# Experts' transpositions in two groups per expert instead of four, the next expert's places worked out a stage earlier, the last output scattered in two halves

## The chip, the cores and the metric

One core of one Trainium2 chip runs the kernel. The metric is the device time of one execution in microseconds; three timed executions of the kernel before gave 1836.58 to 1839.4 us with a median of 1838.2 us.

## The reference

One layer over 1024 tokens of width 1024: a modulated RMS norm, a projection to 2576 columns, an mLSTM mixer and a dilated attention mixer beside each other, an output projection with a gated residual, and then the part that this change concerns:

```
h2 = rms_norm(x, norm2_g) * (1 + scale2) + shift2
affinity = softmax(h2 @ w_router + b_router)
gates, idx = top_k(affinity.T, 128)             # each of 16 experts chooses 128 of 1024 tokens
xin = h2[idx]                                   # 128 x 1024 for each expert
hid = silu(xin @ w_gate) * (xin @ w_up)         # 128 x 2048
y = (hid @ w_down) * gates
out = x + gate2 * zeros.at[idx].add(y)
```

All is float32. Each expert has three weight matrices of 8 MB, so 403 MB are read from device memory for the 16 experts.

## The kernel before, in words

The first 680 us or so compute the mixers, the router and the choice of tokens. The rest, `phase_experts` (L1584), goes through the 16 experts one after the other, and the change lies wholly in it.

**The products.** A weight matrix comes in eight pieces of 128 x 2048 numbers through a ring of buffers, loaded by the SP queue (`feed`, L1474 and L1476). ScalarE rounds a piece to the matrix type (`wh`, L1489) and VectorE takes the rest (`wl`, L1505), so that three products, of the rounded input with `wh`, of the input's rest with `wh` and of the rounded input with `wl`, give nearly float32. `mm` (L1510) issues the 12 matmuls of a piece (L1524), each 128 x 128 by 128 x 512, and then the next cut. There are four buffers each for `wh` and `wl`, and the cut runs about three pieces ahead in the written order. An expert has 24 pieces: 8 for `w_gate`, 8 for `w_up`, 8 for `w_down`, together 288 matmuls.

**The order of the stages.** While expert e is in hand, TensorE does gate(e), up(e), and then down(e-1), which is one expert late. PSUM is two sets of four banks, `px` and `py`, whose roles change with each expert: gate(e) fills set X, up(e) fills set Y, down(e-1) uses two banks of X.

**What stands between the products.** Three small jobs are put between pieces. `expert_hT` (L1556) turns one quarter of the previous expert's hidden rows, by four 128 x 128 transpositions on TensorE (L1564) and a split on ScalarE (L124) and VectorE (L125); it is called after pieces 1, 3, 5 and 7 of gate. `expert_xT` (L1530) turns half of the next expert's gathered rows by four transpositions (L1538), four ScalarE scalings (L1544) and a split; it is called after pieces 2 and 4 of down. `route_expert` (L1429) finds the next expert's places: VectorE writes a one-hot table (`onehot`, L1426), TensorE does eight narrow products (L1437), VectorE makes the list of rows and the gates (L1441 to L1443), and GpSimd starts an indirect DMA that gathers the rows into `xin` (L1445). Its first part follows piece 0 of up, its second part piece 2 of up.

**The output.** At the end of down, VectorE writes the gated result over `xin` in two halves of 512 columns (L1580), and GpSimd starts an indirect DMA that adds its 128 rows of 4 KB to `out` (L1581). `xin` is one buffer: the next gather waits until this scatter has read it, and each scatter to `out` is ordered behind the landing of the one before it, since their rows are known only at run time. At the very end, down of the last expert runs alone and its scatter is the last work of the program.

**What sets the order in the queues.** The functions state an order, but a planner fixes each engine's instruction list before the program runs. It goes through the instructions with assumed costs and takes, whenever an engine is free, the ready one that comes first in the written order; so a transposition whose input is ready can be moved ahead of a product whose weights are not, by its assumed times. The `wl` cuts and the one-hot table keep their written order among themselves (`keep_in_program_order`). On the chip every engine then takes its list strictly in order. The transpositions and places of which the prediction speaks are such instructions.

Of the kernel before, what the change touches and what calls it, by code (L numbers as in the profile page):

```python
# [14 lines left out]
I32 = mybir.dt.int32  # L15
AF = mybir.ActivationFunctionType
OP = mybir.AluOpType
# [3 lines left out]
P = 128  # L21
# [8 lines left out]
NE = 16  # L30
# [16 lines left out]
FEEDS = (2, 8, 14, 20, 26, 32)  # L47
LATE = 3
CUTS = 4
HT = (1, 3, 5, 7)  # L50
PAIR0 = 2, 4, 5
MIX = 8
SORTS = {9: (0, 3), 24: (3, 2), 39: (5, 2)}
# [53 lines left out]
class K:  # L107
# [1045 lines left out]
    def phase_out(self):  # L1153
# [4 lines left out]
        with ExitStack() as st:  # L1158
# [55 lines left out]
            for k in range(MH):  # L1214
                if k == MH - 1:
                    for _ in merge:
                        pass
                prep(k)
                if k == 1:
                    for i in range(NT):  # L1220
                        x_load(i)
                for n in range(2 * G1):
                    mm(pss[n], n // 2, n % 2, k)
                    next(consts, 1)
                    if n % 2:
                        next(merge, 1)
# [23 lines left out]
            for i in range(G1, NT):  # L1250
                for c in range(2):
                    ps = psum()
                    for k in range(MH):
                        mm(ps, i, c, k)
                        step += 1
                        for g in todo.pop(step, ()):
                            g()
                        if step in SORTS:
                            side.append(self.route_sort(*SORTS[step]))
                        if step in FEEDS:  # L1260
                            self.feed()
                        pump(PUMP)
                    epilogue(i, c, ps)
                if i < NT - 1:
                    finish(i, self.out_norm(i, 1, ss), (step + TAIL[0], step + TAIL[1]))
# [163 lines left out]
    def route_expert(self, e, psum):  # L1429

        nc, rt = self.nc, self.rt
        if e:
            self.onehot(e, self.slot)
        oh = self.oh
        ps = psum()
        for i in range(NT):
            nc.tensor.matmul(ps[:, :5], oh[:, i], self.R[:, i, e], start=(i == 0), stop=(i == NT - 1))  # L1437
        yield
        idx = rt.tile([P, 1], I32, name="idx", bufs=3)
        rg = rt.tile([P, 5], F32, name="rg", bufs=3)  # L1440
        nc.vector.tensor_copy(rg, ps[:, :5])  # L1441
        nc.vector.scalar_tensor_tensor(idx, rg[:, 0:1], float(P), rg[:, 1:2], op0=OP.mult, op1=OP.add)
        nc.vector.tensor_reduce(rg[:, 0:1], rg[:, 2:5], axis=AX.X, op=OP.add)  # L1443
        xin = self.xin
        nc.gpsimd.indirect_dma_start(out=xin, out_offset=None, in_=self.h2_d,  # L1445
                                     in_offset=bass.IndirectOffsetOnAxis(ap=idx[:, :1], axis=0))
        yield dict(idx=idx, gate=rg[:, 0:1], xin=xin)
# [62 lines left out]
    def mm(self, xs, n, first, last):  # L1510

        nc = self.nc
        w, l = self.ready.pop(0)
        (xh, xl), ps = xs, n
        N = len(ps) * 512
        prods = (xh, w), (xl, w), (xh, l)
        order = [(q, t, c) for q in range(3) for t in range(FF // N) for c in range(len(ps))]
        if last and not (self.fed or self.halves or self.ready):

            order.sort(key=lambda a: (a[1], a[0], a[2]))  # L1520
        for q, t, c in order:
            x, y = prods[q]
            o = t * N + c * 512
            nc.tensor.matmul(ps[c], x[:, t], y[:, o:o + 512], start=first and q == 0 and t == 0, stop=last and (q, t) == (2, FF // N - 1))  # L1524
        if self.ahead:
            self.ahead -= 1
        else:
            self.cut()
# [36 lines left out]
        self.split(h, l, ps.rearrange("p (k n) -> p k n", k=4))  # L1565
        u.setdefault("hT", []).append((h, l))

    def expert_down(self, u, psum):

        nc = self.nc  # L1570
        ps = [psum() for _ in range(2)]
        for i in range(8):
            h, l = u["hT"][i // 2]
            k = slice(2 * (i % 2), 2 * (i % 2) + 2)
            self.mm((h[:, k], l[:, k]), ps, i == 0, i == 7)
            yield i
        y = self.xin
        for c in range(2):
            t = slice(c * 512, (c + 1) * 512)
            nc.vector.scalar_tensor_tensor(y[:, t], ps[c], u["gate"], self.gate2[:, t], op0=OP.mult, op1=OP.mult)  # L1580
        nc.gpsimd.indirect_dma_start(out=self.out, out_offset=bass.IndirectOffsetOnAxis(ap=u["idx"][:, :1], axis=0),  # L1581
                                     in_=y, in_offset=None, compute_op=OP.add)

    def phase_experts(self):  # L1584


        nc = self.nc
        sets = [lambda: self.psx.tile([P, 512], F32, name="px"), lambda: self.psy.tile([P, 512], F32, name="py")]

        self.hid = self.m2.tile([P, FF], F32, name="hid")  # L1590
        self.xT = (self.sort_mem, self.m1.tile([P, KT, P], F32R, name="xTh", bufs=2),
                   self.yp.tile([P, KT, P], F32R, name="xTl", tag="og", bufs=MH))
        half = lambda pool, tag, **kw: pool.tile([P, D], F32, name="w_half", tag=tag, **kw)
        og = lambda: half(self.yp, "og", bufs=MH)
        self.feed([self.hid], once=True)
        self.feed([half(self.m1, t, bufs=2) for t in ("xTh", "xin")])
        self.xin = self.m1.tile([P, D], F32, name="xin", bufs=2)
        for _ in range(2):
            self.feed([half(self.yap, "ya", bufs=MH) for _ in range(2)], once=True)
        late = [None] * (RING - EARLY) + [[og(), og()], [og(), half(self.m2, "w_x")]]  # L1600
        for t in late[:-LATE]:
            self.feed(t)
        _, u = self.route_expert(0, sets[1])
        for t in late[-LATE:]:
            self.feed(t, nc.gpsimd)
        for _ in range(CUTS - 1):
            self.cut()
        for b in range(2):
            self.expert_xT(u, b, sets[1], True)
        self.started = True  # L1610
        self.ahead = 1
        self.cut()
        p = None
        for e in range(NE):
            X, Y = sets[e % 2], sets[1 - e % 2]
            n = None
            for i in self.expert_up(u, "w_gate", X):
                if p and i in HT:
                    self.expert_hT(p, HT.index(i), Y)
            u["hid"] = hid = self.m2.tile([P, FF], F32, name="hid")  # L1620
            for c in range(4):
                nc.scalar.activation(hid[:, c * 512:(c + 1) * 512], u["ps_w_gate"][c], AF.Silu)  # L1622
            for i in self.expert_up(u, "w_up", Y):
                if e + 1 < NE and i == 0:
                    route = self.route_expert(e + 1, X)
                    next(route)
                if e + 1 < NE and i == 2:
                    n = next(route)
            for c in range(4):
                t = slice(c * 512, (c + 1) * 512)  # L1630
                nc.vector.tensor_mul(hid[:, t], hid[:, t], u["ps_w_up"][c])
            if p:
                for i in self.expert_down(p, X):
                    if n and i in (2, 4):
                        self.expert_xT(n, i // 2 - 1, Y)
                    if e == NE - 1 and i in (2, 4, 6):
                        self.expert_hT(u, i // 2 - 1, Y)
            elif n:
                for b in range(2):
                    self.expert_xT(n, b, Y)  # L1640
            p, u = u, n
        self.expert_hT(p, 3, Y)
        for _ in self.expert_down(p, Y):
            pass


# [100 lines left out]
```

## Time and profile before

| | |
|---|---|
| median of three timed executions | 1838.2 us (1836.58 to 1839.4) |
| the profiled execution: its own time, its span | 1833.95 us, 1832.0 us |
| TensorE matmul busy, over the span | 1722.9 us (94%) |
| VectorE busy | 1487.1 us (81%) |
| ScalarE busy | 1197.7 us (65%) |
| GpSimd busy | 180.5 us (10%) |
| DMA | 517.26 MB, mean 282 GB/s |
| mean granted TensorE clock | 0.982 of full |

The shares are means over the mixers, the router and the experts together. In the page's 40 slices the experts are the last 25: TensorE shows 9 tenths or more in nearly all of them, VectorE 8 or 9, ScalarE 6 or 7, and the DMA engines 9. Three engines and the DMA are all near their limit there, so what bounds an expert has to be read from the waits inside it.

### The profile page before, as it was taken

What the parts mean: (1) busy time and instruction counts of PE and PEld (TensorE: products, weight loads), DVE (VectorE), ACT (ScalarE), POOL (GpSimd) and SP (SyncE); (2) the same over time, 40 slices, a digit from 0 to 9 for tenths busy, and PEclk for the clock granted to TensorE, in tenths of its full rate; (3) what the DMA queues carried; (4) which work ended last, traced back from release to release, by engine and by line L of the source; (5) the groups of instructions that cost most, each with busy time, mean ns of one, the idle gap of its engine ahead of it and who ended that gap; (6) DMA issues with size and microseconds to landing.
All of it is one profiled execution on the core that took longest, in us unless ns stands there. A gap on an engine that the chain in (4) does not pass through costs nothing. (4 is left out here: it accounts for less than half of the span.)

```text
span 1832.0 us, 24429 instructions
## 1 busy us (share of the span) xinstructions
PE 1722.9 (94%) x8696; PEld 1402.8 (77%) x8696; DVE 1487.1 (81%) x2156; ACT 1197.7 (65%) x1603; POOL 180.5 (10%) x185
## 2 busy tenths in 40 slices
PE   5999999989998939999999999999999999999997
PEld 4777888778886827888888778777787777777785
DVE  5578885687866788988988898888898888888886
ACT  5346454377763537787777777776776776777764
POOL 1001000031123020010110000100000001001000
PEclk9999999999999959999999999999999999999999
DMA  9135663325557768999999999999999999999892
GB/s 325 42 114 172 213 215 98 110 80 116 135 129 227 258 255 336 359 354 382 410 363 345 373 345 379 372 335 390 352 369 384 357 364 387 329 382 368 311 391 67
DMA packets 152553, 517.26 MB, mean 282 GB/s; under 512 B 33163, under 2 KB 50833, under 8 KB 116721
## 3 DMA queue, kind: packets, MB, share of 16 engines
q1 hardware_dynamic: 138560, 478.92, 70.7%
q0 software_dynamic: 10960, 36.32, 7.5%
q8 instruction: 68, 1.11, 0.2%
q10 hardware_dynamic: 2912, 0.48, 0.2%
q14 instruction: 53, 0.43, 0.1%
HBM read 488.16 MB, written 27.50 MB: 281 GB/s over the span
## 5 line engine op out<-in xcount | busy, mean ns | idle before, releaser
L1505 DVE TENSOR_TENSOR wl<-w,wh 128x2048 fp32r<-128x2048 f32 x278 | 627.8, 2285 | 81.6 <-ACT wh L1489 81.2
L1489 ACT ACTIVATE wh<-w 128x2048 fp32r<-128x2048 f32 x278 | 523.1, 1919 | 55.2 <-PE py L1524 26.3
L1505 DVE TENSOR_TENSOR wl<-w_half,wh 128x1024 fp32r<-128x1024 f32 x210 | 245.6, 1217 | 8.6 <-ACT wh L1489 8.5
L1489 ACT ACTIVATE wh<-w_half 128x1024 fp32r<-128x1024 f32 x210 | 211.8, 1058 | 24.1 <-PE px L1524 13.1
L1524 PE MATMUL py<-wl,xTh 128*128 128x512 f32 x512 | 139.9, 394 | 7.7 <-DVE wl L1505 7.7
L1524 PE MATMUL px<-wl,xTh 128*128 128x512 f32 x512 | 139.7, 394 | 4.5 <-DVE wl L1505 4.5
L1524 PE MATMUL px<-wh,xTh 128*128 128x512 f32 x512 | 141.1, 395 | 2.3 <-ACT xTh L124 2.1
L1524 PE MATMUL py<-wh,xTh 128*128 128x512 f32 x512 | 140.8, 394 | 2.2 <-ACT wh L1489 2.0
L1524 PE MATMUL py<-wh,xTl 128*128 128x512 f32 x512 | 138.3, 390 | 0.0
L1524 PE MATMUL px<-wh,xTl 128*128 128x512 f32 x512 | 138.1, 391 | 0.0
L1524 PE MATMUL px<-wh,hT 128*128 128x512 f32 x512 | 130.4, 396 | 0.1
L1524 PE MATMUL py<-wh,hT 128*128 128x512 f32 x512 | 129.0, 393 | 0.0
L1524 PEld LDWEIGHTS py<-wl,xTh 128*128 128x128 f32 x512 | 94.6, 188 | 33.4 <-DVE wl L1505 14.6
L1524 PEld LDWEIGHTS px<-wl,xTh 128*128 128x128 f32 x512 | 95.0, 188 | 29.5 <-DVE wl L1505 10.4
L1524 PEld LDWEIGHTS px<-wh,xTh 128*128 128x128 f32 x512 | 95.3, 189 | 23.9 <-ACT xTh L124 2.5
L1524 PEld LDWEIGHTS py<-wh,xTh 128*128 128x128 f32 x512 | 94.7, 188 | 24.0 <-ACT wh L1489 4.5
L1524 PEld LDWEIGHTS px<-wh,hT 128*128 128x128 f32 x512 | 95.6, 190 | 22.1 <-ACT wh L1489 2.1
L1524 PEld LDWEIGHTS px<-wh,xTl 128*128 128x128 f32 x512 | 96.7, 189 | 20.6
L1524 PEld LDWEIGHTS py<-wh,xTl 128*128 128x128 f32 x512 | 96.0, 188 | 20.4 <-DVE xTl L125 0.2
L1524 PEld LDWEIGHTS py<-wh,hT 128*128 128x128 f32 x512 | 95.0, 188 | 20.8 <-ACT wh L1489 0.7
L1581 POOL DMA_INDIRECT out_dram<-xin,idx x16 | 48.3, 3019 | 590.6 <-DVE xin L1580 590.6
L1445 POOL DMA_INDIRECT xin<-h_d,idx x16 | 37.8, 2362 | 477.9 <-DVE rg L1443 197.4
(456 smaller groups left out, 3138.2 us busy)
## 6 DMA issues: line engine op xcount, KB each, us to landing
w<-in_w_down_dram SPq DMA_DIRECT2D x95, 1024.0 KB, 8.4
w<-in_w_gate_dram SPq DMA_DIRECT2D x91, 1024.0 KB, 7.2
w<-in_w_up_dram SPq DMA_DIRECT2D x88, 1024.0 KB, 7.1
w_half<-in_w_gate_dram SPq DMA_DIRECT2D x70, 512.0 KB, 7.6
w_half<-in_w_up_dram SPq DMA_DIRECT2D x70, 512.0 KB, 7.5
w_half<-in_w_down_dram SPq DMA_DIRECT2D x66, 512.0 KB, 8.3
ada_w<-in_w_ada_dram SPq DMA_DIRECT2D x64, 256.0 KB, 3.5
wraw<-in_w_in_dram SPq DMA_DIRECT2D x20, 512.0 KB, 4.3
```

Source lines behind the costliest of these rows:

```text
L1445: nc.gpsimd.indirect_dma_start(out=xin, out_offset=None, in_=self.h2_d, in_offset=bass.IndirectOffsetOnAxis(ap=idx[:, :1], axis=0))
L1489: act = self.nc.scalar.activation(h[:, j * m:(j + 1) * m], t, AF.Copy)
L1505: self.tc.keep_in_program_order(self.nc.vector.tensor_sub(l[:, c], t, h[:, c]))
L1524: nc.tensor.matmul(ps[c], x[:, t], y[:, o:o + 512], start=first and q == 0 and t == 0, stop=last and (q, t) == (2, FF // N - 1))
L1581: nc.gpsimd.indirect_dma_start(out=self.out, out_offset=bass.IndirectOffsetOnAxis(ap=u["idx"][:, :1], axis=0), in_=y, in_offset=None, comp ...
```

## The change

`HT` becomes a table from piece to quarters: after piece 3 of gate the quarters 0 and 1 of the previous hidden rows are turned, after piece 6 the quarters 2 and 3. Both halves of the next input are turned after piece 3 of down. The one-hot table of the next expert is written after piece 1 of gate instead of after piece 0 of up, its eight products come after piece 3 of gate, right behind the first group of transpositions and in the other PSUM set, and the row list and the gather after piece 5 of gate instead of piece 2 of up. For the last expert all four quarters are turned inside down of the one before, after its pieces 3 and 6, where a quarter had come after it. In the very last piece the 12 products are sorted by output half first, and each half of the result is scattered by a DMA of its own, 128 rows of 2 KB each, to the row numbers 2*idx and 2*idx+1 of `out` seen as 2048 half rows; VectorE makes these numbers.

```
-HT = (1, 3, 5, 7)
+HT = {3: (0, 1), 6: (2, 3)}
...
     def route_expert(self, e, psum):
-        if e:
-            self.onehot(e, self.slot)
...
-            order.sort(key=lambda a: (a[1], a[0], a[2]))
+            order.sort(key=lambda a: (a[2], a[0], a[1]))
...
-    def expert_down(self, u, psum):
+    def expert_down(self, u, psum, last=False):
...
             nc.vector.scalar_tensor_tensor(y[:, t], ps[c], u["gate"], self.gate2[:, t], op0=OP.mult, op1=OP.mult)
-        nc.gpsimd.indirect_dma_start(out=self.out, ...)
+            if last:
+                row = self.rt.tile([P, 1], I32, name="idx", bufs=3)
+                nc.vector.tensor_scalar(row, u["idx"], 2.0, float(c), op0=OP.mult, op1=OP.add)
+                nc.gpsimd.indirect_dma_start(out=self.out.rearrange("s (h n) -> (s h) n", h=2), ..., in_=y[:, t], compute_op=OP.add)
+        if not last:
+            nc.gpsimd.indirect_dma_start(out=self.out, ...)
...
             for i in self.expert_up(u, "w_gate", X):
-                if p and i in HT:
-                    self.expert_hT(p, HT.index(i), Y)
+                if p:
+                    for b in HT.get(i, ()):
+                        self.expert_hT(p, b, Y)
+                if e + 1 < NE and i == 1:
+                    self.onehot(e + 1, self.slot)
+                if e + 1 < NE and i == 3:
+                    route = self.route_expert(e + 1, Y)
+                    next(route)
+                if e + 1 < NE and i == 5:
+                    n = next(route)
...
-            for i in self.expert_up(u, "w_up", Y):
-                if e + 1 < NE and i == 0:
-                    route = self.route_expert(e + 1, X)
-                    next(route)
-                if e + 1 < NE and i == 2:
-                    n = next(route)
+            for _ in self.expert_up(u, "w_up", Y):
+                pass
...
                 for i in self.expert_down(p, X):
-                    if n and i in (2, 4):
-                        self.expert_xT(n, i // 2 - 1, Y)
-                    if e == NE - 1 and i in (2, 4, 6):
-                        self.expert_hT(u, i // 2 - 1, Y)
+                    if n and i == 3:
+                        for b in range(2):
+                            self.expert_xT(n, b, Y)
+                    if e == NE - 1:
+                        for b in HT.get(i, ()):
+                            self.expert_hT(u, b, Y)
...
-        self.expert_hT(p, 3, Y)
-        for _ in self.expert_down(p, Y):
+        for _ in self.expert_down(p, Y, True):
             pass
```

## Rows read from the trace of the kernel before

**Rows 1.** Busy time by stretch, one expert each, with its header

```profile
core 0: us, PE busy (x) PEld busy (x) DVE busy (x) ACT busy (x) POOL busy (x), PEclk, DMA share, GB/s
865.18:934.05 68.87, 68.87 (x321) 56.81 (x320) 63.68 (x48) 54.17 (x51) 7.20 (x2) 1.00 0.99 383
...
1148.63:1220.63 72.00, 70.52 (x322) 56.42 (x320) 62.65 (x47) 53.27 (x49) 5.91 (x2) 1.00 0.96 364
...
1651.86:1727.76 75.90, 72.58 (x323) 57.49 (x321) 62.02 (x48) 51.73 (x49) 5.91 (x2) 0.98 0.92 343
```

**Rows 2.** Waits from 780 to 1780 us: total us, times, longest

```profile
DVE wl L1505 <- ACT wh L1489: 80.5, 50, 5.5
...
ACT wh L1489 <- DMA w_half<-in_w_gate_dram: 0.8, 1, 0.8
```

**Rows 3.** TensorE's timeline: start us, us, ..., count; the expert from 934 us

```profile
939.50 0.63 PE L1564 MATMUL py<-ident,hid 128*128 128x128 f32 x4
939.88 1.17 PE L1524 MATMUL px<-wh,xTh 128*128 128x512 f32 x4
940.89 1.08 PE L1524 MATMUL px<-wh,xTl 128*128 128x512 f32 x4
941.81 1.08 PE L1524 MATMUL px<-wl,xTh 128*128 128x512 f32 x4
...
967.42 0.35 PE L1437 MATMUL px<-route_rhs,oh 128*128 128x5 bf16 x8
967.63 0.71 PE L1524 MATMUL py<-wh,xTl 128*128 128x512 f32 x2
968.18 1.09 PE L1524 MATMUL py<-wl,xTh 128*128 128x512 f32 x4
```

**Rows 4.** TensorE's timeline, down and the next gate, from 1126 us

```profile
1125.99 1.03 PE L1538 MATMUL py<-ident,xin 128*128 128x128 f32 x8
1126.78 2.09 PE L1524 MATMUL px<-wh,hT 128*128 128x512 f32 x8
1128.70 0.75 PE L1564 MATMUL px<-ident,hid 128*128 128x128 f32 x5
...
1151.60 1.19 PE L1524 MATMUL py<-wl,xTh 128*128 128x512 f32 x4 [0.99 <-DVE wl L1505]
```

**Rows 5.** TensorE's timeline, two places where it waits for gathered rows

```profile
1554.87 0.52 PE L1538 MATMUL py<-ident,xin 128*128 128x128 f32 x3 [1.55 <-DMA xin<-h_d,idx]
...
1700.34 1.29 PE L1538 MATMUL py<-ident,xin 128*128 128x128 f32 x5 [2.18 <-DMA xin<-h_d,idx]
1701.28 3.24 PE L1524 MATMUL px<-wh,hT 128*128 128x512 f32 x8
```

**Rows 6.** Busy time by stretch, columns as in Rows 1, behind the second wait

```profile
1701.00:1703.00 2.00, 2.00 (x7) 1.71 (x7) 1.20 (x2) 1.55 (x5) 0.00 (x0) 0.50 1.08 383
```

**Rows 7.** DMA issues from 780 to 1730 us, median us from issue to landing

```profile
out_dram<-xin,idx POOLq DMA_INDIRECT x13, 12.2
xin<-h_d,idx POOLq DMA_INDIRECT x13, 10.2
```

**Rows 8.** GpSimd's timeline: a scatter inside the loop and the last one

```profile
1654.64 3.39 POOL L1581 DMA_INDIRECT out_dram<-xin,idx  x1 [32.47 <-DVE xin L1580]
...
1821.31 1.57 POOL L1581 DMA_INDIRECT out_dram<-xin,idx  x1 [20.21 <-DVE xin L1580]
```

**Rows 9.** VectorE groups from 800 to 1832 us: count, busy us, mean ns

```profile
L1505 DVE TENSOR_TENSOR wl<-w,wh 128x2048 fp32r<-128x2048 f32 x248 | 559.7, 2285 | 73.8 <-ACT wh L1489 73.7
...
L1426 DVE TENSOR_TENSOR oh<-iota,slot 128x1024 bf16<-128x1024 f32 x13 | 15.8, 1218 | 0.0
```

**Rows 10.** VectorE's timeline, the last result

```profile
1819.44 1.41 DVE L1580 SCALAR_TENSOR_TENSOR xin<-px,rg,gate 128x512 f32<-128x512 f32 x2 [4.11 <-PE px L1524]
```

**Rows 11.** The chain that ended last, merged in order of time, near its end

```profile
1799.53 6.17 DMA out_dram<-xin,idx
```

**Rows 12.** Busy time by stretch, columns as in Rows 1, the last scatter's bytes

```profile
1823.00:1827.00 4.00, 0.00 (x0) 0.00 (x0) 0.00 (x0) 0.00 (x0) 0.00 (x0) 0.53 0.88 131
```

More of the change, by code (lines that the diff above doesn't have):

```diff
@@ L1580, in expert_down @@
             nc.vector.scalar_tensor_tensor(y[:, t], ps[c], u["gate"], self.gate2[:, t], op0=OP.mult, op1=OP.mult)
-        nc.gpsimd.indirect_dma_start(out=self.out, out_offset=bass.IndirectOffsetOnAxis(ap=u["idx"][:, :1], axis=0),
-                                     in_=y, in_offset=None, compute_op=OP.add)
+            if last:
+                row = self.rt.tile([P, 1], I32, name="idx", bufs=3)
+                nc.vector.tensor_scalar(row, u["idx"], 2.0, float(c), op0=OP.mult, op1=OP.add)
+                nc.gpsimd.indirect_dma_start(out=self.out.rearrange("s (h n) -> (s h) n", h=2), out_offset=bass.IndirectOffsetOnAxis(ap=row[:, :1], axis=0),
+                                             in_=y[:, t], in_offset=None, compute_op=OP.add)
+        if not last:
+            nc.gpsimd.indirect_dma_start(out=self.out, out_offset=bass.IndirectOffsetOnAxis(ap=u["idx"][:, :1], axis=0),
+                                         in_=y, in_offset=None, compute_op=OP.add)
     def phase_experts(self):
```

## The prediction

> **What bounds the kernel now.** I read first the busy times cut by expert, then the waits inside the expert stage, then TensorE's own timeline, and the chain only for its end. The first shows two kinds of expert. The one from 865 us takes 68.87 us with TensorE busy throughout; the one from 1148 us, which stands for the nine or so later ones without another disturbance, takes 72.00 us with the same 288 products; the one from 1651 us takes 75.90 us and its mean clock is 0.98 [rows 1]. The reader is to see that the DMA share is as high in the quick expert (0.99) as in the others, so the high share alone doesn't mark a limit. The waits say the same: ScalarE waits for a weight piece once, for 0.8 us, in the longest such row, while VectorE waits 80.5 us in 50 pieces for ScalarE's rounded half [rows 2]. So TensorE bounds the stage, and where it loses time the cut of the weights has lost its lead: at the start of a gate stage TensorE sits 0.99 us before the third product [rows 4].
>
> The timeline then shows that the written places of the small jobs hold only in the early experts. There, four transpositions stand by themselves between pieces [rows 3]. In the expert from 1076 us the planner has already put all eight transpositions of the next input in one row, near the start of down, and the first five of the hidden rows three microseconds behind them, in down rather than in the next gate [rows 4]. The change writes groups that for these experts exist in part already.
>
> **The change part by part.** The sum is made against the profiled execution, 1833.95 us (span 1832.0 us).
>
> *Fewer groups.* The transpositions and narrow products stay the same in number; only the breaks between them and the wide products go. A group of four costs 939.88 - 939.50 = 0.38 us, and the four wide products behind it take 1.01 us against 0.92 us for the next four: 0.09 us for the break [rows 3]. Two such groups cost 0.94 us. A group of eight takes 0.79 us, and the eight products behind it take 1.92 us against 1.84 us by the same 0.92 us for four: 0.87 us together [rows 4]. A merge saves about 0.07 us. The eight narrow products of the places take 0.21 us, and the two products behind them 0.55 us instead of 0.46 us [rows 3]; put behind transpositions they lose that 0.09 us. With two merges of hidden rows, one of input rows and the places, an expert gains 3 x 0.07 + 0.09 = 0.30 us, over 15 experts 4.5 us if the written order is kept. I take 0.30 us for three early experts and 0.1 us for the twelve others, where the planner's own order decides: -2.1 us, with ends at 0 and -4.5 us.
>
> *The places a stage earlier.* The gather is now asked for after piece 5 of gate, before after piece 2 of up. That is five pieces of 12 products, 5 x 2.76 = 14 us, by 0.92 us for four [rows 3]. Twice the gather was late: TensorE waited 1.55 and 2.18 us for it [rows 5]. Behind the second wait the granted clock was 0.50, the 1.2 GHz level [rows 6], and eight products took 3.24 us where they take 2.09 us behind an ordinary group [rows 4, 5]: 1.15 us more. A gather lands 10.2 us after its issue in the median [rows 7], so 14 us more lead removes both waits whole: -1.55 - 2.18 - 1.15 = -4.9 us. The new place could meet the previous scatter, which reads the same buffer: that is issued 2.8 us into the expert and lands 12.2 us later in the median [rows 1, 7, 8], at about 15 us, and the gather is wanted at about 6 x 2.76 = 17 us. GpSimd has nothing queued behind it in that stage, and even a wait of some microseconds leaves the gather ahead of its need in down, some 30 us on.
>
> *VectorE's share of the places.* The one-hot table costs VectorE 1.22 us [rows 9]. It keeps its place among the cuts, now between the cuts for gate pieces 4 and 5, before between those for up pieces 3 and 4. A cut takes 2.29 us [rows 9] and TensorE needs a piece every 2.76 us, so VectorE gains 0.47 us a piece; after the lead was lost at the start of gate [rows 4], the five cuts ahead of the table have regained 2.3 us, less 0.7 us or so for each hidden quarter that is split meanwhile (estimated at the 0.7 us that half of the two-part result of the last rows takes [rows 10]). That covers 1.22 us, barely. In up the same table is gone from a stretch that begins with VectorE waiting for ScalarE [rows 2], which gains nothing certain. I take 0. The far ends: all 1.22 us open in eleven late experts, +13 us; and the 0.99 us wait, of which there is about one per late expert, shortened by a third, -4 us.
>
> *The end.* Sorted by halves, the first half is complete six products before the last one instead of one before, 5 x 0.23 = 1.2 us sooner, and its scatter need not wait for the second result of 0.7 us [rows 10]: it can be issued 1.9 us sooner, at 1819.4 instead of 1821.31 us [rows 8]. In the chain the last scatter hangs on the landing of the scatter before it [rows 11]; both add to rows known at run time. I expect the second half to be held back in the same way, until the first has landed. The last scatter's bytes move from 1823 to 1827 us [rows 12], 1.7 us after issue. With half the bytes I take 1.7 + 2.0 us for each half and 0.3 us to land and reissue: 1819.4 + 3.7 + 0.3 + 3.7 = 1827.1 us, against 1827: with 0.6 us for the two extra row-number instructions and for 2 KB rows that move less well, +0.7 us. If the halves weren't ordered, the bytes would start 1.9 us sooner, -1.9 us; if each half took the 6.17 us of a whole scatter [rows 11], 1819.4 + 6.2 + 5.7 = 1831.3 us, +4.3 us.
>
> The Trainium skill's page "DMA: Bandwidth & Descriptors", section "Anatomy of one DMA — SWDGE (gpsimd) path", gives about 2.0 us fixed plus the bytes at 436 GB/s for one such DMA, which speaks against halving. The last scatter shows 131 GB/s instead [rows 12], so the bytes count for more here than the page has it. By the page, as an estimate, two halves of 0.26 MB cost 5.2 us against 3.2 us for one, so +0.1 us after the 1.9 us of head start, and the sum below would be 0.6 us lower.
>
> Together -2.1 - 4.9 + 0 + 0.7 = -6.3 us, or 1827.65 us for a run like the profiled one. That run is 4.25 us under the median of those timed, so against the median I forecast 1838.2 - 6.3 = 1831.9 us.
>
> **The rivals.** *Slower: the table in gate (0.21).* If the planner leaves two or more hidden splits in gate ahead of the table, VectorE's lead at that point is under 1.22 us and TensorE waits there in every late expert. For it speaks that the lead is nil at the start of gate and that nothing but the difference of 0.47 us a piece restores it; against it, that hidden quarters are already turned in down [rows 4]. It decides from the second split on; at 11 x 1.22 = 13 us, less the 6.3 us, the time is 1845 us.
>
> *Hidden anyway (0.20).* The gather comes in time but the waits move: the input's eight ScalarE scalings wait for down as before, and the lost lead returns as another 1 to 2 us wait at the same two experts; the groups stay as the planner has them. Then only the end differs, 1836 to 1841 us, 1838.5 us in the middle. For it speaks that the late experts lose 3.1 us over the early one with no late gather at all [rows 1].
>
> *The early order returns (0.08).* If the earlier gather and the larger groups let the planner keep the written order throughout, eleven late experts would drop by 72.00 - 68.87 = 3.1 us [rows 1], 34 us beside the 4.9: 1800 us. Against it speaks that the small jobs are moved because the planner sees TensorE idle, and the change gives it no more weights.
>
> **How the numbers follow.** The forecast has 0.51, its own range is 1826 to 1837 us. The bound of what can be told from no change is 0.2%, 3.7 us: 1834.5 and 1841.9 us. Of the forecast 0.42 lies below, 0.09 within; the early order adds 0.08 below; of the hidden case 0.02 lies below, 0.15 within and 0.03 above; the table is 0.21 above. Faster 0.52, same 0.24, slower 0.24. The range of 1812 to 1848 us leaves out most of the early order, and the upper end of the +13 and +4 us.
>
> **What would show it.** Right: no wait of TensorE on the gather after 700 us, the gather issued some 14 us sooner after the start of its expert, no clock of 0.50 before the end, and two last scatters about 4 us apart. The table's cost shows as waits of TensorE on `wl` in the middle of gate; the fewer breaks as groups of eight and more. Wrong: late experts still at 72 us and over without a late gather gone, new waits at piece 5 of gate, or late experts far from 72 us on either side, which would mean that the planner's order, and not the terms above, set the time.

## The result, and the profile after

The changed kernel takes 1888.51 us (median of four runs, 1885.66 to 1892.84) against 1837.39 us for the kernel before (four runs, 1836.13 to 1839.4): the ratio is 1.0282, with a 95% interval of 1.0266 to 1.0298. I had forecast 1831.9 us in a range of 1812 to 1848 us. The profiled execution has a span of 1883.5 us, 51.5 us over the one before.

The busy times from the page (engine, us, share of the span, instructions) are nearly those of before for VectorE and ScalarE, so they don't do more work; the kernel stands still more. TensorE's 16 us more go with a lower mean clock (0.970 against 0.982). GpSimd's 40 us more, 220.9 against 180.5 us, are the instructions that start the scatters; they come back at the end of this text:

```profile
PE 1739.0 (92%) x8696; PEld 1413.2 (75%) x8696; DVE 1482.5 (79%) x2158; ACT 1198.6 (64%) x1603; POOL 220.9 (12%) x186
```

Two waits of VectorE are new, from the waits of the changed kernel (us in total, times, longest):

```profile
DVE idx L1440 <- DMA out_dram<-xin,idx: 35.7, 8, 8.3
...
DVE idx L1582 <- DMA out_dram<-xin,idx: 11.6, 2, 8.1
```

VectorE waits for a scatter before it writes a list of rows. L1440 is the line that makes the row list `idx` in `route_expert` (L1442 before), L1582 the new line that makes the half-row numbers. The list of expert e+1 is a new tile under the name `idx`, which has three buffers; it takes the one that held the list of expert e-2. The scatter of e-2 reads that list for its destinations, and it is issued at the start of gate(e). Before, the next list was made in up, long after it had landed. Now it is made in gate. VectorE runs its list in order, so every cut behind the row list waits as well, as the last two rows below show. VectorE's timeline (start, duration, line, [idle before]) shows it in the expert from 1681 us:

```profile
1691.77 1.22 DVE L1426 TENSOR_TENSOR oh<-iota,slot 128x1024 bf16<-128x1024 f32 x1
1694.47 0.17 DVE L1439 COPY rg<-py 128x5 f32<-128x5 f32 x1 [1.48 <-PE py L1435]
1702.62 0.16 DVE L1440 SCALAR_TENSOR_TENSOR idx<-rg 128x1 int32<-128x1 f32 x1 [7.99 <-DMA out_dram<-xin,idx]
1702.82 0.16 DVE L1441 TENSOR_REDUCE rg<-rg 128x1 f32<-128x3 f32 x1
1702.90 2.29 DVE L1503 TENSOR_TENSOR wl<-w,wh 128x2048 fp32r<-128x2048 f32 x1
```

Its inputs are there at 1694.64 us, 13.3 us into the expert; it runs at 1702.62 us. The cut right behind it is the one that TensorE waits for, in its own timeline:

```profile
1697.52 0.27 PE L1562 MATMUL py<-ident,hid 128*128 128x128 f32 x1
1705.24 2.08 PE L1522 MATMUL px<-wl,xTh 128*128 128x512 f32 x4 [7.45 <-DVE wl L1503]
1707.12 1.91 PE L1522 MATMUL px<-wh,xTh 128*128 128x512 f32 x4
1708.82 1.91 PE L1522 MATMUL px<-wh,xTl 128*128 128x512 f32 x4
```

After 7.45 us without work the next groups of four take 1.7 to 1.9 us from start to start instead of 0.9. The busy times by stretch (columns as in [rows 1]) give the granted clock as 0.50, the 1.2 GHz level, for these 8 us, and 82.35 us for the whole expert, 6.45 us over the slowest one of before [rows 1]:

```profile
1681.38:1763.73 82.35, 74.18 (x327) 59.07 (x326) 61.46 (x48) 50.07 (x48) 13.77 (x2) 0.94 0.86 316
1703.00:1711.00 8.00, 5.76 (x14) 4.55 (x15) 8.00 (x6) 0.00 (x0) 2.52 (x1) 0.50 0.59 222
```

The chain of waits names the same scatter, 19.33 us from its issue to its landing, and the list and the cut right behind it:

```profile
1683.19 19.33 DMA out_dram<-xin,idx
1702.90 2.30 DVE wl L1503
1705.24 8.85 PE px L1522 x25
```

The end has the mechanism twice more, on VectorE and TensorE by their timelines. The half-row numbers are tiles under the name `idx` too:

```profile
1782.70 0.15 DVE L1582 TENSOR_SCALAR idx<-idx 128x1 int32<-128x1 int32 x1 [8.05 <-DMA out_dram<-xin,idx]
...
1853.74 0.15 DVE L1582 TENSOR_SCALAR idx<-idx 128x1 int32<-128x1 int32 x1 [3.57 <-DMA out_dram<-xin,idx]
```

```profile
1785.16 2.07 PE L1522 MATMUL py<-wl,xTh 128*128 128x512 f32 x4 [7.24 <-DVE wl L1503]
...
1856.16 1.20 PE L1522 MATMUL px<-wl,hT 128*128 128x512 f32 x4 [2.38 <-DVE wl L1503]
```

The planner put the first of them 86 us ahead of the scatter that uses it, 10.6 us behind another scatter's issue (1772.13 us).

### The profile page after: what moved, and what is told of

Its sections match the earlier page's. It is cut to its first block, busy times and chain, and to the rows that moved or that the text cites. A ratio compares the mean times of both kernels' runs of the same rounds, so it can differ in the third digit from the quotient of the medians.

```text
span 1883.5 us, 24430 instructions
## 1 busy us (share of the span) xinstructions
PE 1739.0 (92%) x8696; PEld 1413.2 (75%) x8696; DVE 1482.5 (79%) x2158; ACT 1198.6 (64%) x1603; POOL 220.9 (12%) x186
## 3 DMA queue, kind: packets, MB, share of 16 engines
q1 hardware_dynamic: 138560, 478.92, 68.9%
## 4 chain that ended last, share of the span: by engine, by line
PE 30%; DVE 8%; DMA 7%; ACT 4%; issue 3%; POOLq 0%; DVEq 0%; ACTq 0%
PE py L1522 17%; PE px L1522 12%; DVE wl L1503 7%; DMA out_dram<-xin,idx 4%; ACT wh L1487 3%; DMA w<-in_w_up_dram 1%; DMA w_half<-in_w_up_dram 1%; ACT sort_mem L1542 1%; DVE hT L125 0%; DVE xin L1578 0%; DVE xTl L125 0%; DMA w<-in_w_down_dram 0%; DMA w<-in_w_gate_dram 0%; PE px L1562 0%; PE px L1536 0%
## 5 line engine op out<-in xcount | busy, mean ns | idle before, releaser
L1586 POOL DMA_INDIRECT out_dram<-xin,idx x15 | 86.2, 5744 | 831.1 <-DVE xin L1578 831.1
L1522 PE MATMUL px<-wl,xTh 128*128 128x512 f32 x512 | 144.8, 405 | 21.0 <-DVE wl L1503 21.0
L1522 PE MATMUL py<-wl,xTh 128*128 128x512 f32 x512 | 142.0, 397 | 14.6 <-DVE wl L1503 14.5
L1522 PEld LDWEIGHTS py<-wl,xTh 128*128 128x128 f32 x512 | 95.3, 190 | 39.7 <-DVE wl L1503 20.6
L400 PE MATMUL pa<-wh,hTh 128*128 128x512 f32 x192 | 79.5, 415 | 0.9 <-ACT wh L357 0.6
```

The lines of the kernel that those rows point to most:

```text
L400: nc.tensor.matmul(ps, hTh[:, k, t], hi[k], start=(k == 0), stop=False)
```

## The experiments

Theory: the row list's buffer. Rivals: the one-hot table in gate, which had been my slower case, and the larger groups. Each ratio is against runs of the kernel before in the same session; the medians of these lie between 1837.12 and 1839.05 us.

**One more buffer.** `a_idx4_rows` is the changed kernel with

```
-        idx = rt.tile([P, 1], I32, name="idx", bufs=3)
+        idx = rt.tile([P, 1], I32, name="idx", bufs=4)
...
-                row = self.rt.tile([P, 1], I32, name="idx", bufs=3)
+                row = self.rt.tile([P, 1], I32, name="row", bufs=2)
```

> The changed kernel with a fourth buffer for the row list idx and two buffers of their own for the last half-row numbers; all else as changed. Theory (index buffer): VectorE stands still because the row list of expert e+1 takes the buffer of expert e-2, whose scatter is still under way in gate, and in order behind it stand the cuts; with a free buffer the waits of VectorE on the scatter (47 us in all) go to 0, TensorE's long waits on wl (2.6 to 7.5 us) with them, and the time comes back to 1830 to 1842 us. Rival 1 (table in gate): the one-hot table and the row list in gate take VectorE's lead by themselves; the time stays over 1865 us. Rival 2 (large groups): eight transpositions at once and their splits hold ScalarE and VectorE up; the time stays over 1865 us too.

1839.08 us, ratio to before 1.0007 (0.9998 to 1.0017). Both waits are gone from VectorE's list. In the same expert as above, now from 1657 us, the row list follows the places at once:

```profile
1666.95 1.22 DVE L1426 TENSOR_TENSOR oh<-iota,slot 128x1024 bf16<-128x1024 f32 x1
1669.65 0.17 DVE L1439 COPY rg<-py 128x5 f32<-128x5 f32 x1 [1.48 <-PE py L1435]
1669.85 0.16 DVE L1440 SCALAR_TENSOR_TENSOR idx<-rg 128x1 int32<-128x1 f32 x1
```

49.4 of the 51.1 us were the buffers. Both rivals had said 1865 us or more: neither makes the loss by itself.

**The end alone.** `a_rows_own` has only the second of these two edits.

> The changed kernel with two buffers of their own for the last half-row numbers only; the row lists of the loop keep three. Theory (index buffer): the last two waits of VectorE (8.05 and 3.57 us) go, with the TensorE waits behind them (7.24 and 2.38 us) and the low clock after the first; about 12 to 15 us less, 1872 to 1878 us. Rivals 1 and 2: no change, 1886 to 1892 us.

1876.68 us, 1.0202 (1.0185 to 1.0219). The two waits at the end cost 1888.51 - 1876.68 = 11.8 us, those in the loop 1876.68 - 1839.08 = 37.6 us. The split is rough, since the loop isn't quite the same: VectorE's waits for the scatter in it are 41.6 us in six places here, 35.7 us in eight in the changed kernel.

**The parts one by one, on the kernel before.** `b_places` moves only the table, the places, the list and the gather; `b_groups` has only the groups of eight.

In `b_places`:

```
-        if e:
-            self.onehot(e, self.slot)
...
+                if e + 1 < NE and i == 1:
+                    self.onehot(e + 1, self.slot)
+                if e + 1 < NE and i == 3:
+                    route = self.route_expert(e + 1, Y)
+                    next(route)
+                if e + 1 < NE and i == 5:
+                    n = next(route)
...
```

In `b_groups`:

```
-HT = (1, 3, 5, 7)
+HT = {3: (0, 1), 6: (2, 3)}
...
-                    if n and i in (2, 4):
-                        self.expert_xT(n, i // 2 - 1, Y)
+                    if n and i == 3:
+                        for b in range(2):
+                            self.expert_xT(n, b, Y)
...
```

> The kernel before with one part of the change: the one-hot table, the places' products, the row list and the gather at their new points in gate; groups and end as before. Theory (index buffer): the loop's waits on the scatter come back, 25 to 40 us more than before, 1862 to 1878 us. Rival 1 (table in gate): the same time, but the waits of TensorE stand behind the table and not behind the scatter. Rival 2 (large groups): 1832 to 1840 us.

> The kernel before with one part of the change: the transpositions in groups of eight (hidden rows after pieces 3 and 6 of gate, input rows after piece 3 of down); places, gather and end as before. Theory (index buffer): no wait on a scatter, 1832 to 1840 us. Rival 1: the same. Rival 2 (large groups): 1860 us or more.

`b_places` takes 1892.4 us, ratio 1.028 (1.0255 to 1.0306): the move alone gives the whole loss, and more than I expected, since VectorE waits 52.3 us where the changed kernel's list waits 35.7 (in the late experts in which it waits, it reaches the list 3 to 10 us after the scatter's issue here, 10 to 12 us in the changed kernel):

```profile
DVE idx L1440 <- DMA out_dram<-xin,idx: 52.3, 9, 8.9
```

`b_groups` takes 1837.32 us, 0.999 (0.9978 to 1.0003): no difference that can be told. Its waits show that the late gathers stay when the gather stays in up:

```profile
PE py L1538 <- DMA xin<-h_d,idx: 3.8, 2, 2.3
```

**The same move with a free buffer.** `b_places_idx4` is `b_places` with `bufs=4` for `idx`.

> The kernel before with the places and the gather at their new points in gate, and a fourth buffer for the row list; against the same without the fourth buffer (1892.4 us) the one number shows what the buffer costs. Theory (index buffer): no wait of VectorE on a scatter and no wait of TensorE on the gather; back to 1833 to 1840 us, that is some 55 us less. If the table in gate (rival 1) had a cost of its own of 10 us and more, 1843 us or over.

1830.09 us, 0.9963 (0.9948 to 0.9978). One buffer of one number per partition turns +55 us into -7 us. TensorE's wait for the gather is gone, and a table in gate that cost 10 us doesn't exist. GpSimd now meets the scatter instead, with nothing queued behind it:

```profile
POOL xin L1443 <- DMA out_dram<-xin,idx: 20.5, 2, 10.8
```

**The end in two halves, by itself.** `b_tail_own` is the kernel before with the sorted last piece and the two scatters, their numbers in buffers of their own (`name="row", bufs=2`).

> The kernel before with the end alone changed: products of the last piece sorted by halves, two scatters, the half-row numbers in buffers of their own. Theory: the second scatter is held until the first has landed, about 5 us after its issue as in the changed kernel with free buffers, so the program ends 3 to 4 us later, 1840 to 1841.5 us; my forecast's term was +0.7 us, 1838 us.

1841.18 us, 1.0020 (1.0007 to 1.0033), 3.9 us slower by the medians and between 1.3 and 6.1 us by the interval. From the first product of the last down to the end of the program the trace has 37.8 us against 34.9 us before, 2.9 us more. GpSimd's timeline shows the second half held until the first has landed:

```profile
1819.18 1.57 POOL L1585 DMA_INDIRECT out_dram<-xin,row  x1 [18.90 <-DVE xin L1580]
1824.86 1.55 POOL L1585 DMA_INDIRECT out_dram<-xin,row  x1 [4.11 <-DMA out_dram<-xin,row]
```

**The change without its end.** `a_idx4_whole` is `a_idx4_rows` with the last output scattered whole and the last piece in its old order.

> The changed kernel with a fourth buffer for the row list and with the last output scattered whole, as before. Theory: what is left of the change is the two late gathers (-5 us), the breaks in the early experts (-1 us) and the table in gate in the late ones (+2 to +5 us): 1833 to 1837 us, some 3.5 us less than with the two scatters.

1835.55 us, 0.9991 (0.9982 to 1.0001). The two scatters cost 3.5 us here by the medians and again 2.9 us by the traces of the two (38.0 against 35.1 us from the first product of the last down). What is left of the change can't be told from nothing, and it is 5.5 us slower than the move alone.

**A later list.** `a_list_late` is `a_rows_own` with the list after piece 7:

```
-                if e + 1 < NE and i == 5:
+                if e + 1 < NE and i == 7:
                     n = next(route)
```

> The kernel of a_rows_own (three buffers for the row list, own buffers for the last half-row numbers) with the row list and the gather after piece 7 of gate instead of piece 5, two pieces or 5.5 us later. Theory (index buffer): the waits of VectorE on the scatter (41.6 us in six places, 9.3 us at most) shrink by 5.5 us each, to some 10 us in all, and the time falls from 1876.7 to 1840 to 1852 us. If something else in gate than the scatter's landing held VectorE, moving the list would change little: 1870 us or more.

1866.68 us, 1.016 (1.0136 to 1.0183): 10 us less instead of 25 to 37. VectorE's waits for the scatter fall from 41.6 us in six places to 26.6 us in five. The expectation missed, because the written point holds only where the planner keeps it. In the second early expert the list comes with no wait (6.15 us in `a_rows_own`); in three late ones, which hold 25.7 of the 26.6 us, the planner still runs it as soon as its inputs are ready, with a scatter under way that lands only 19.0 to 19.3 us after its issue. Of two experts:

```profile
895.63 0.16 DVE L1440 SCALAR_TENSOR_TENSOR idx<-rg 128x1 int32<-128x1 f32 x1
...
1249.16 0.16 DVE L1440 SCALAR_TENSOR_TENSOR idx<-rg 128x1 int32<-128x1 f32 x1 [9.30 <-DMA out_dram<-xin,idx]
```

**The written order, held.** Since the late experts take 72 us where the early ones take 68.5, I held the instructions of TensorE, ScalarE and VectorE in the expert stage in their written order, all but the three short ones of VectorE that make the row list and the gates, each as here:

```
-            nc.tensor.matmul(ps[c], x[:, t], y[:, o:o + 512], ...)
+            self.tc.keep_in_program_order(nc.tensor.matmul(ps[c], x[:, t], y[:, o:o + 512], ...))
```

`a_pinned` does this to `a_idx4_whole`, `b_pinned` to the kernel before, `b_places_pinned` to `b_places_idx4`; `a_pinned_idx3` is `a_pinned` with three buffers again.

> The kernel of a_idx4_whole, and every instruction of TensorE, ScalarE and VectorE in the expert stage held in its written order, so that the planner moves none of them. Theory: the late experts take 71 to 73 us instead of 68.5 because their small jobs were moved and the cut of the weights lost its lead; in the written order all take 68.5 us, 11 x 3.3 = 36 us less, 1800 us. Rival: the DMA or VectorE sets the 72 us, and the order changes nothing or makes it worse: 1835 us or more.

> The kernel before, nothing of the change, with every instruction of TensorE, ScalarE and VectorE in the expert stage held in its written order. Theory: the gain of a_pinned (1804.8 us) is nearly all from the order; the gathers are early enough in the written order or cost some us; 1803 to 1812 us. If the change's earlier gather and larger groups were needed for it, 1820 us or more.

> The kernel of b_places_idx4 (places and gather at the new points in gate, fourth buffer, small groups, whole scatter) in its written order. Theory: what the held order needs is the two pieces between the one-hot table and its products and the free buffer, not the large groups; late experts at 68.8 us as the early ones, four breaks more than in a_pinned at 0.07 us, 1805 to 1812 us. If the large groups were needed to keep the cut's lead, experts of 70 us and more and 1825 us or over.

> The kernel of a_pinned with three buffers for the row list instead of four. Theory (index buffer): in the written order the list comes at the same point of every expert, so VectorE waits for the scatter in each as in the changed kernel's early experts (3.2, 5.3 and 4.6 us), TensorE 2 to 4.5 us behind it: 14 times 3 to 5 us with the low clock, 1850 to 1875 us.

`a_pinned` takes 1804.76 us, 0.9819 (0.9804 to 0.9833): faster than both kernels. The thirteen experts from 806 to 1699 us now take 68.5 to 69.1 us each. Two of them, by stretch, with TensorE never idle at a DMA share as high as ever:

```profile
1012.51:1080.99 68.48, 68.48 (x322) 57.09 (x320) 62.14 (x47) 53.75 (x49) 5.37 (x2) 1.00 0.96 376
1356.01:1424.72 68.71, 68.71 (x321) 57.01 (x320) 63.33 (x48) 53.63 (x49) 10.61 (x2) 1.00 0.98 390
```

`b_pinned` takes 1907.01 us, 1.0373 (1.0354 to 1.0392); I had expected 1803 to 1812. In TensorE's timeline two waits return in every expert:

```profile
843.35 0.63 PE L1568 MATMUL py<-ident,hid 128*128 128x128 f32 x4
843.74 0.94 PE L1528 MATMUL py<-wh,xTh 128*128 128x512 f32 x3
845.65 0.50 PE L1528 MATMUL py<-wh,xTh 128*128 128x512 f32 x1 [0.97 <-DVE hT L125]
...
851.89 0.36 PE L1440 MATMUL px<-route_rhs,oh 128*128 128x5 bf16 x8 [3.90 <-DVE oh L1429]
```

The table and its products are written at one point in up, but VectorE's list is about three cuts ahead of TensorE there. The table stands behind these cuts, of which the last had itself waited 2.81 us for ScalarE, and TensorE waits 3.90 us for it. And the last hidden quarter is turned after piece 7 of gate, so its PSUM bank isn't read out when the first product of up wants it: 0.97 us. `b_places_pinned` removes the first wait by the change's two pieces between table and products, and keeps the second: 1820.44 us, 0.9895 (0.9865 to 0.9925), with

```profile
PE px L1526 <- DVE hT L125: 7.5, 8, 1.0
PE py L1526 <- DVE hT L125: 6.6, 7, 1.0
```

I had expected 1805 to 1812 us: the groups matter after all, since the change's last group comes after piece 6. Whether their size counts beside their place isn't shown. `a_pinned_idx3` takes 1916.21 us, 1.0405 (1.0374 to 1.0437), 111 us over the same with four buffers, and 41 us over the upper end of what I expected:

```profile
DVE idx L1445 <- DMA out_dram<-xin,idx: 101.9, 13, 11.0
```

The wait now comes in 13 places and is 7.8 us long on average, not 3 to 5. The list itself wasn't held, so it doesn't come at one point: VectorE reaches it 7.5 to 15.5 us after the scatter's issue, and the scatters land 13.1 to 21.4 us after it.

## Why the prediction was wrong, step by step

*The places a stage earlier: this step failed.* I asked what the earlier gather could meet, looked at `xin` alone, found the scatter landed "at about 15 us" and the gather wanted at "6 x 2.76 = 17 us", and put the wait on GpSimd, which "has nothing queued behind it". That part was right: GpSimd waits and nobody minds, as `b_places_idx4` shows. But the scatter reads two things, the rows in `xin` and the row list in `idx`, and the list has its own three buffers. I didn't ask who last used the buffer that the moved instruction writes. The writer is VectorE, with the cuts queued behind. The rows at hand would have told half of it: a scatter issued 2.8 us into the expert that lands 12.2 us later [rows 1, 7, 8] frees the buffer at 15 us, and the list, four pieces of 2.76 us into gate, can be ready from 12 us on. I expected it after piece 5; in some late experts, as in the one from 1681 us, it was due right behind the products after piece 3, since the planner takes it once its inputs are ready. Twelve places by 3 us would have been a forecast on the right side, but partly by luck; the runs have eight waits of 0.4 to 8.3 us in the loop, 35.7 us together, and 37.6 us of time with the low clock behind them.

The other half is the landing time. I took 12.2 us, the median of the kernel before. In the changed kernel five scatters of the loop land 18.6 to 20.6 us after their issue, and 29.4 of the 35.7 us of waits stand behind these five. In the three early experts VectorE comes to the list 15.5 to 16.5 us after the scatter's issue; behind a landing of 12.2 us, or of the 14.3 to 14.6 us that the same three took before, none of them would have waited. From VectorE's timeline of the changed kernel, four of the five, in the experts from 800, 871, 947 and 1386 us:

```profile
826.63 0.16 DVE L1440 SCALAR_TENSOR_TENSOR idx<-rg 128x1 int32<-128x1 f32 x1 [3.24 <-DMA out_dram<-xin,idx]
...
897.50 0.16 DVE L1440 SCALAR_TENSOR_TENSOR idx<-rg 128x1 int32<-128x1 f32 x1 [5.30 <-DMA out_dram<-xin,idx]
...
973.88 0.16 DVE L1440 SCALAR_TENSOR_TENSOR idx<-rg 128x1 int32<-128x1 f32 x1 [4.55 <-DMA out_dram<-xin,idx]
...
1408.71 0.16 DVE L1440 SCALAR_TENSOR_TENSOR idx<-rg 128x1 int32<-128x1 f32 x1 [8.27 <-DMA out_dram<-xin,idx]
```

The late landings need the shared buffer to do harm: `a_idx4_rows` has them too (19.4 to 21.4 us) and no wait.

*The two late gathers* went as forecast: -4.9 us foreseen, and the move as a whole gives 7.2 us (4.0 to 9.6 by the interval) once the buffer is free. In `a_idx4_rows` the expert that had taken 75.90 us takes 71.89 us.

*VectorE's share of the places*, at 0, holds within what can be told. The rival of the table in gate had the right engine, stage and sign, and a wrong cause: the move with a free buffer is faster than before.

*Fewer groups* gained 0.3 to 0.4 us in each early expert as the sum said (68.5 against 68.9 us), and nothing in the late ones. Together with the moved places the late experts lost some of the gathers' gain (1835.55 against 1830.09 us). Why is open; the planner's order differs in every one of them, and I have no run that tells which difference counts.

*The end* was mis-sized: +0.7 us, of a possible +4.3; it measured +3.9 and +3.5 by the medians, +2.9 in both traces. I took each half for 3.7 us, with 0.3 us more to land and issue the next, so the second 4 us behind the first. A half takes 4.9 us to land, a whole scatter 6.17 [rows 11], and the second half starts 5.7 us behind the first. And its half-row numbers, which I counted as "two extra row-number instructions", cost 11.8 us by the buffers that they took.

*The early order returns* was given 0.08 and 1800 us. It didn't return by the change, but held by hand it gives 1804.76 us: what the late experts lose is order, neither DMA nor VectorE. How much of the 3.6 us by which the first two experts of `a_pinned` are slower than before (120.6 against 117.1 us, from the first product to that of the third gate) could be had back wasn't tried.

## What to carry to other kernels

When an instruction moves earlier, follow every tile that it writes to the last reader of the buffer it takes; with rotating buffers that reader may be a DMA of three rounds ago, and the wait falls on the engine that writes, with all that is queued there. Price that wait with the spread of the DMA's landings (9.2 to 20.6 us within one kernel's loop here), not with the median of the kernel before. A tile of 512 bytes deserves a spare buffer before anything else is reordered. And where a planner orders the queues, a written place is only a wish: read from the trace where an instruction runs, or hold it, and then leave every producer as many steps ahead of its consumer as its own queue runs ahead.

## What was not expected of the hardware

The landing of one and the same scatter, 128 rows of 4 KB added to device memory, is far from constant: 6.17 us at the end with the other queues silent, 12.2 us in the median within the loop of before, 14.6 us in the changed kernel and 19.9 us in `a_pinned`, as the median of the DMA issues shows:

```profile
out_dram<-xin,idx POOLq DMA_INDIRECT x14, 19.9
```

Two things go with it. One is the company: counted from the end of GpSimd's own instruction, a scatter lands 7 to 11.5 us later in the loops of these three kernels, where the DMA share meanwhile is 0.92 or more, and 4.3 to 4.7 us later at the end, beside no other transfer. The other is that instruction, which is most of the difference between the kernels. GpSimd's timeline of the changed kernel:

```profile
806.91 11.29 POOL L1586 DMA_INDIRECT out_dram<-xin,idx  x1 [52.43 <-DVE xin L1578]
...
1612.34 3.37 POOL L1586 DMA_INDIRECT out_dram<-xin,idx  x1 [55.06 <-DVE xin L1578]
1683.19 11.25 POOL L1586 DMA_INDIRECT out_dram<-xin,idx  x1 [53.05 <-DVE xin L1578]
```

The first and the last of these land after 19.6 and 19.3 us, the one between after 12.3 us. Before, the instruction takes 1.6 to 5.7 us; in the changed kernel 11.1 to 11.3 us in five experts; in `a_pinned` 8.9 to 11.3 us in twelve of fourteen. The larger groups have a part in it: in `b_groups` the first three scatters take GpSimd 10.0 to 10.2 us instead of 5.6 to 5.7 us and land after 18.1 to 20.5 us, with no wait of VectorE behind them, while in `b_places` they are as before. So in the early experts the groups make the scatter land late, and the moved list makes it matter. Why the instruction takes longer, no run here shows.

Halving its bytes at the end shortened the landing only from 6.17 to 4.9 us.
